# Feed-forward blocks but the first: the row of reciprocal roots by memory instead of by transposes, and tile 0 gated behind tile 1's sums

## The chip, the cores and the metric

The kernel runs on one core of one Trainium2 chip. The metric is the device time of one execution in microseconds. The engines are named as in the profile: PE is TensorE (PEld its weight loads), DVE is VectorE, ACT is ScalarE, POOL is GpSimd, SP is SyncE, whose queue issues nearly all transfers here.

## What is computed

Two layers of a decoder trunk for 256 tokens of width 1024, in float32. Each layer is a feed-forward half step, a mixer of three groups of attention heads, and a second feed-forward half step:

```python
def rms_norm(x, g):
    xf = x.astype(jnp.float32)
    y = xf * lax.rsqrt(jnp.mean(xf * xf, axis=-1, keepdims=True) + RMS_EPS)
    return (y * g.astype(jnp.float32)).astype(x.dtype)

def swiglu(x, w_gate, w_up, w_down):
    return (jax.nn.silu(x @ w_gate) * (x @ w_up)) @ w_down

for l in range(DEPTH):
    h = h + 0.5 * swiglu(rms_norm(h, ffn1_norm[l]), ffn1_w_gate[l], ffn1_w_up[l], ffn1_w_down[l])
    h = h + hybrid_mixer(rms_norm(h, mix_norm[l]), w_in[l], ...)
    h = h + 0.5 * swiglu(rms_norm(h, ffn2_norm[l]), ffn2_w_gate[l], ffn2_w_up[l], ffn2_w_down[l])
```

The hidden width of the feed-forward steps is 2816. So there are four feed-forward blocks in a run: two per layer, with the mixer between the two of a layer. The reciprocal root in `rms_norm` is one number per token; it is what the change carries in another way.

## The kernel before

**Weights.** Each matrix product in float32 is made from pieces in a rounded format: a weight unit of 128 x 1024 values is loaded raw, ScalarE makes its high part `wh` (L118) and VectorE the rest `wl` (L122). Transfers of 1 MB go into five `raw` buffers (`RAW_BUFS`); a buffer's next load is issued by SyncE (L92) as soon as both units in it are split. Up to eight split units are kept. `W.pump()` emits the next split of each kind, and where it stands in the program is where the split stands in the queues of ScalarE and VectorE. The order on each engine is the order of the program; there is no scheduler (`manual_schedule`).

**Feed-forward block.** The hidden width is cut into 22 tiles of 128 columns (`NF`). For each tile a `Pair` of PSUM banks takes the gate and the up product, hidden columns on the partitions and the 256 tokens along the free axis. `wide` is eight matmuls with `wh` on 512 columns for each of the two banks, `narrow` eight with `wl` on 256 columns; odd tiles do the narrow ones first (`swapped`). The banks have four buffers, so tile f + 2 takes the banks of tile f. `summed` (L441 on ScalarE, L442 on VectorE) adds the two halves of a bank and so frees it. Then `gated` multiplies by the reciprocal roots `norm.rb` (L446, VectorE) and takes the tanh (L448, ScalarE); `silu` is two operations of VectorE (L465, and L466 with `rb` again); `hidden` multiplies by the up half (L453), makes the high part `hh` (L456, ScalarE) and the rest `hl` (L459, VectorE). The down product of tile f - 4 is done in the loop at tile f (`DOWN_LAG`), in four `acc` banks.

**The norm.** The products run on the input that is not yet divided by its root mean square; the reciprocal roots come in at `gated` and `silu`. Squares are summed while the first products run. `norm.sums` (L358, L313 on VectorE, L314 on GpSimd) gives `self.r`, named `y_n` in the profile: token p of half t on partition p, column t. The tiles need it along the free axis and on all partitions, as `rb`, 128 x 256. `norm.broadcast` does that: two transposes on TensorE of a column of `y_n` spread over 128 columns (L364), and a copy from PSUM by ScalarE (L366).

**Head of a block.** Tiles 0 and 1 start together, `p0` and `p1`, while the second half of the input is still turned (L338). Then: `norm.sums`, the rest of `p0`, `summed` of tile 0, the rest of `p1`'s wide products, `norm.broadcast`, `p1`'s narrow products, and then tile 0 is gated, before the loop over tiles 1 to 21 begins; tile 1's sums are taken as its first step. `W.pump()` stands between the steps of tile 0. The first block of the run (`first`) has an opening of its own; the other three share this head.

Of the kernel before, what the change touches and what calls it, by code (L numbers as in the profile page):

```python
# [10 lines left out]
F32 = mybir.dt.float32  # L11
# [7 lines left out]
P = 128  # L19
S = 256  # L20
# [122 lines left out]
def kernel(ctx: ExitStack, tc: tile.TileContext, x, ffn1_norm, ffn1_w_gate, ffn1_w_up, ffn1_w_down,  # L143
                      mix_norm, w_in, forget_bias, a_q_norm, a_k_norm, b_q_norm, b_k_norm, c_q_norm, c_k_norm,
                      w_out, ffn2_norm, ffn2_w_gate, ffn2_w_up, ffn2_w_down, const, out):
    nc = tc.nc
# [3 lines left out]
    xp = ctx.enter_context(tc.tile_pool(name="xp", bufs=1))  # L150
# [2 lines left out]
    sm = ctx.enter_context(tc.tile_pool(name="sm", bufs=4))  # L153
    at = ctx.enter_context(tc.tile_pool(name="at", bufs=1))
    pp = ctx.enter_context(tc.tile_pool(name="pp", bufs=2))
    psum = ctx.enter_context(tc.tile_pool(name="psum", bufs=4, space=PSUM))
    ctx.enter_context(tc.manual_schedule())

# [2 lines left out]
    def bank(tag):  # L161
        return psum.tile([P, 512], F32, name="ps_" + tag, tag=tag)

    def tmp(n):
        return tp.tile([P, 512], F32, name="tmp", tag="tmp")[:, :n]
# [39 lines left out]
    W = Weights(tc, raw_pool, split_pool)  # L205
# [74 lines left out]
    def load_small():  # L280
        nc.sync.dma_start(cst, const)
        load_gains(1, mix_norm, nc.sync)
        load_gains(2, ffn2_norm, nc.sync)
        nc.sync.dma_start(fb, bass.AP(tensor=forget_bias.tensor, offset=forget_bias.offset,
                                      ap=[[0, P], [8, DEPTH], [1, 8]]))
# [19 lines left out]
    def mm3(o, lhs, rhs, start, stop):  # L305
        mm(o, lhs[0], rhs[0], start, False)
        mm(o, lhs[0], rhs[1], False, False)
        mm(o, lhs[1], rhs[0], False, stop)
# [8 lines left out]
    class Norm:  # L317
# [43 lines left out]
        def broadcast(self):  # L361
# [3 lines left out]
            self.rb = xp.tile([P, S], F32, name="rb", tag="rb")  # L365
            A.copy(self.rb, ps[:, :S])  # L366

    def tokens(o, q, hid, w, start, stop, cols=slice(0, 512)):

        t, c = q % 2, q // 2  # L370
        mm3(o, [h[:, t * P:(t + 1) * P] for h in hid], [v[:, 0, 512 * c + cols.start:512 * c + cols.stop] for v in w],
            start, stop)
# [8 lines left out]
    def ffn(norm, nxt, aside=None, first=False):  # L381
        hid = {}

        def down(k):
            w = W.take()
            for q in range(4):
                tokens(acc[q], q, hid[k], w, k == 0, False)
            del hid[k]

        def finish(ks):  # L390
            ws = [(k, W.take()) for k in ks]
            dst = out[0].rearrange("(t p) d -> p t d", p=P)
            for q in range(4):
                for c in ((0, 512),) if q < 3 else ((0, 256), (256, 512)):
                    c = slice(*c)
                    o = bank("gu")[:, :S] if c.start else acc[q][:, c]
                    if c.start:
                        residual(q, acc[q][:, c], 0.25, c)
                    for k, w in ws:
                        tokens(o, q, hid[k], w, c.start > 0 and k == ks[0], k == ks[-1], c)  # L400
                    d = residual(q, o, 0.25, c)
                    at = 512 * (q // 2) + c.start
                    nc.sync.dma_start(dst[:, q % 2, at:at + c.stop - c.start], d)
# [34 lines left out]
        def summed(ps):  # L438

            o = tmp(S)  # L440
            A.copy(o, ps[:, 1])  # L441
            V.tensor_tensor(o, ps[:, 0], o, op=ALU.add)  # L442
            return o

        def gated(t_):
            V.tensor_tensor(t_, t_, norm.rb, op=ALU.mult)  # L446
            th = tmp(S)
            A.activation(th, t_, AF.Tanh, scale=0.5)  # L448
            return t_, th

        def hidden(f, t_, th, u, pumps=1):
            late = f >= NF - 2
            V.tensor_tensor(t_, u, t_, op=ALU.mult)  # L453
            hh = hp.tile([P, S], F32R, name="hh", tag="hh")
            hl = hp.tile([P, S], F32R, name="hl", tag="hl")
            (V.tensor_copy if late else A.copy)(hh, t_)  # L456
            if not late:
                W.pump(pumps)
            V.tensor_tensor(hl, t_, hh.bitcast(F32), op=ALU.subtract)  # L459
            if late:  # L460
                W.pump(pumps)
            hid[f] = (hh, hl)

        def silu(t_, th):
            V.scalar_tensor_tensor(t_, th, 1.0, t_, op0=ALU.add, op1=ALU.mult)  # L465
            V.tensor_tensor(t_, t_, norm.rb, op=ALU.mult)  # L466
# [87 lines left out]
            p1.both(lo)  # L554
        W.pump()
        norm.sums()
        (g0, u0), (g1, u1) = p0.both(hi), p1.ps
        W.pump()
        g0, u0 = summed(g0), summed(u0)
        W.pump()  # L560
        p1.wide(hi)
        norm.broadcast()
        p1.narrow(hi)
        W.pump()
        t_, th = gated(g0)
        if not first:
            W.pump()
        silu(t_, th)
        hidden(0, t_, th, u0, int(not first))
        acc = [bank("acc") for _ in range(4)]  # L570
        for f in range(1, NF):
            last = f == NF - 1
            def lagging():
                if DOWN_LAG <= f != NF - 2:
                    down(f - DOWN_LAG - last)

            if f == 1:
                g, u = g1, u1
            elif f % 2:
                g, u = Pair().swapped(lagging)  # L580
            else:
                p = Pair()
                p.wide(range(KT))
                lagging()
                p.narrow(range(KT))
                g, u = p.ps
            if last:
                W.pump()
            g = summed(g)
            if not last:  # L590
                u = summed(u)
            t_, th = gated(g)
            if last:
                W.low()
                down(f - DOWN_LAG)
            else:
                W.pump()
                if f == 1:
                    lagging()
                if f >= DOWN_LAG:  # L600
                    W.pump()
            silu(t_, th)
            hidden(f, t_, th, summed(u) if last else u, 3 if last else 1 + (first and f in (2, 3)))
            if f == 4 and first:
                load_small()
            if f == 8 and aside:
                aside()
# [3 lines left out]
    def tail(acc, rhs, ks, factor, make_norm, late=None):  # L611

        nxt = make_norm()
        ws = dict(zip(ks, [W.take() for _ in ks]))

        def part(q, some):
            for k in some:
                tokens(acc[q], q, rhs[k], ws[k], False, k == ks[-1])  # L620

        ahead = [0] * 4
        if late:
            part(0, ks[:2])
            part(1, ks[:1])
            late()
            part(1, ks[1:2])
            part(2, ks[:1])
            ahead = [2, 2, 1, 0]
        for q in range(4):  # L630
            part(q, ks[ahead[q]:])
            residual(q, acc[q], factor)
            if q == 2:
                nxt.half(0)
        W.pump()
        return nxt
# [548 lines left out]
    def before_mixer(l):  # L1185
        if l == 0:
            turn_gains(1)
            turn_gains(2)
            V.tensor_copy(identr, ident)
            V.memset(causal[:, P:2 * P], 0.0)  # L1190
            for t in range(2):
                V.tensor_scalar(causal[:, 2 * t * P:(2 * t + 1) * P], future, NEG, None, op0=ALU.mult)
        mixer_tables(l)
# [8 lines left out]
    norm = Norm(0, 0)  # L1202
    turn_gains(0)
    for l in range(DEPTH):
        norm = ffn(norm, lambda: Norm(1, l), lambda: before_mixer(l), l == 0)
        norm = mixer(l, norm, lambda: Norm(2, l))
        norm = ffn(norm, (lambda: Norm(0, l + 1)) if l + 1 < DEPTH else None)
# [35 lines left out]
```

## Time and profile before

| What | us |
|---|---|
| median of 3 runs | 1037.53 |
| lowest and highest run | 1037.35, 1038.41 |
| profiled execution | 1037.25 |
| span of the profiled execution | 1035.5 |
| PE busy | 1031.3 |
| DVE busy | 808.0 |
| ACT busy | 592.1 |
| POOL busy | 147.3 |

The profile is one execution. Its page gives the busy time of each engine, the granted clock of TensorE in 40 slices (9 is full), and the chain that ended last, followed back from the last instruction. The timeline gives instructions in order of time: start and length in microseconds, engine, line, operation, destination and source, count, and in brackets the idle time of the engine just before and what ended it. Instructions that follow each other and are alike stand in one row with a count, so the length of such a row is that of the group. Matmuls are pipelined and overlap: the distance between starts, not the length, is what one costs. The rows of transfers give count, size, and the time from issue to landing.

### The profile page before, as it was taken

How to read it: one execution, taken by the hardware profiler on the slowest of the kernel's cores; microseconds unless marked ns; L12 is line 12 of the kernel's file. 1: busy time of each engine (PE TensorE's matmuls, PEld its weight loads, DVE VectorE, ACT ScalarE, POOL GpSimd, SP SyncE). 2: the span in 40 equal slices, each digit the busy share in tenths (PEclk: the TensorE clock that was granted, in tenths of full speed). 3: DMA queues.
4: the chain of work that ended last, by engine and by line, in shares of the span. 5: the costliest groups of instructions: out<-in, count | busy, mean ns of one | idle time of the engine just before them, and what ended most of it. 6: DMA issues, size and time to landing. Idle time of an engine off the chain costs nothing.

```text
span 1035.5 us, 15082 instructions
## 1 busy us (share of the span) xinstructions
PE 1031.3 (100%) x5641; PEld 898.4 (87%) x5641; DVE 808.0 (78%) x1537; ACT 592.1 (57%) x1045; POOL 147.3 (14%) x177
## 2 busy tenths in 40 slices
PE   9999999999999999999999999999999999999998
PEld 8888888898888888888888888888988988888887
DVE  6977778789876877777788777787898768777776
ACT  6655556666854655555465555557676646555552
POOL 2003000167800000000000110002766000000000
PEclk9999999999999999999999999999999999999999
DMA  9664656554431364645645564664455224564631
GB/s 324 224 240 162 208 188 198 182 191 170 158 127 42 123 230 150 230 168 203 198 163 193 182 224 146 241 186 172 164 195 170 83 69 160 180 204 162 236 130 41
DMA packets 130808, 181.61 MB, mean 175 GB/s; under 512 B 7040, under 2 KB 104624, under 8 KB 130736
## 3 DMA queue, kind: packets, MB, share of 16 engines
q1 hardware_dynamic: 130704, 180.66, 51.3%
q8 instruction: 44, 0.72, 0.3%
q14 instruction: 28, 0.23, 0.1%
q10 hardware_dynamic: 32, 0.01, 0.0%
HBM read 179.60 MB, written 1.05 MB: 174 GB/s over the span
## 4 chain that ended last, share of the span: by engine, by line
PE 100%; DVE 0%; POOL 0%; issue 0%; POOLq 0%
PE ps_gu L303 66%; PE ps_acc L303 30%; PE ps_acc L338 1%; PE ps_gu L1037 1%; PE ps_gu L1140 1%; PE ps_acc L738 0%; PE ps_acc L1037 0%; PE ps_gu L1070 0%; PE ps_acc L495 0%; PE ps_acc L364 0%; PE ps_acc L1070 0%; PE ps_gu L179 0%; DVE trunk L377 0%; POOL ones L183 0%; POOL minus_half L185 0%
## 5 line engine op out<-in xcount | busy, mean ns | idle before, releaser
L122 DVE TENSOR_TENSOR wl<-raw,wh 128x1024 fp32r<-128x1024 f32 (+2 forms) x342 | 417.0, 1225 | 24.7 <-ACT wh L118 24.7
L118 ACT CAST wh<-raw 128x1024 fp32r<-128x1024 f32 (+2 forms) x341 | 343.1, 1036 | 5.4 <-PE ps_gu L303 4.8
L303 PE MATMUL ps_gu<-xhl,wh 128*128 128x512 f32 x1408 | 330.2, 390 | 0.0
L303 PEld LDWEIGHTS ps_gu<-xhl,wh 128*128 128x128 f32 x1408 | 262.7, 188 | 53.8 <-ACT wh L118 0.3
L303 PEld LDWEIGHTS ps_gu<-xhl,wl 128*128 128x128 f32 x1408 | 176.0, 191 | 4.3 <-issue 0.2
L303 PE MATMUL ps_gu<-xhl,wl 128*128 128x256 f32 x1408 | 179.2, 283 | 0.1
L303 PE MATMUL ps_gu<-wh,xhl 128*128 128x512 f32 (+2 forms) x512 | 157.2, 377 | 0.0
L442 DVE TENSOR_TENSOR tmp<-ps_gu,tmp 128x256 f32<-128x256 f32 x176 | 73.0, 423 | 107.8 <-ACT tmp L441 107.5
L303 PE MATMUL ps_acc<-wh,hh 128*128 128x512 f32 (+1 forms) x352 | 137.2, 390 | 0.0
L303 PE MATMUL ps_acc<-wl,hh 128*128 128x512 f32 (+1 forms) x352 | 137.0, 389 | 0.0
L303 PE MATMUL ps_acc<-wh,hl 128*128 128x512 f32 (+1 forms) x352 | 136.5, 388 | 0.0
L441 ACT COPY tmp<-ps_gu 128x256 f32<-128x256 f32 x176 | 63.5, 371 | 93.5 <-PE ps_gu L303 93.2
L303 PEld LDWEIGHTS ps_gu<-wh,xhl 128*128 128x128 f32 x512 | 94.8, 188 | 14.6
L456 ACT CAST hh<-tmp 128x256 fp32r<-128x256 f32 x80 | 32.6, 407 | 119.7 <-DVE tmp L453 119.7
L303 PE MATMUL ps_gu<-wl,xhl 128*128 128x512 f32 (+2 forms) x256 | 95.7, 374 | 0.0
L448 ACT ACTIVATE tmp<-tmp 128x256 f32<-128x256 f32 x88 | 36.9, 419 | 82.3 <-DVE tmp L446 81.9
L314 POOL TENSOR_TENSOR y_n<-msq,minus_half 128x2 f32<-128x2 f32 x6 | 6.8, 1141 | 530.9 <-DVE msq L313 530.9
L303 PEld LDWEIGHTS ps_acc<-wh,hl 128*128 128x128 f32 x352 | 66.1, 188 | 13.9
L303 PEld LDWEIGHTS ps_acc<-wh,hh 128*128 128x128 f32 x352 | 66.2, 188 | 12.6
L303 PEld LDWEIGHTS ps_acc<-wl,hh 128*128 128x128 f32 x352 | 66.2, 188 | 12.2
L303 PEld LDWEIGHTS ps_gu<-wl,xhl 128*128 128x128 f32 x256 | 48.2, 188 | 6.7
L327 ACT ACTIVATE xhl<-ps_acc,gT 128x256 fp32r<-128x256 f32 x48 | 19.1, 474 | 38.7 <-PE ps_acc L338 35.6
(221 smaller groups left out, 1000.4 us busy)
## 6 DMA issues: line engine op xcount, KB each, us to landing
raw<-in_ffn_w_down_dram SPq DMA_DIRECT2D x44, 1024.0 KB, 4.9
raw<-in_ffn_w_gate_dram SPq DMA_DIRECT2D x42, 1024.0 KB, 6.6
raw<-in_ffn_w_up_dram SPq DMA_DIRECT2D x42, 1024.0 KB, 7.3
raw<-in_w_in_dram SPq DMA_DIRECT2D x24, 1024.0 KB, 4.9
raw<-in_w_out_dram SPq DMA_DIRECT2D x8, 1024.0 KB, 4.9
raw<-in_w_in_dram SPq DMA_DIRECT2D x4, 768.0 KB, 4.9
raw<-in_w_in_dram SPq DMA_DIRECT2D x4, 656.0 KB, 3.9
raw<-in_ffn_w_gate_dram SPq DMA_DIRECT2D x3, 512.0 KB, 7.0
```

The costliest lines, as they stand in the source:

```text
L118: self.nc.scalar.copy(hv, src)
L122: (engine or self.nc.vector).tensor_tensor(lv, self.srcs[self.n_low], hv.bitcast(F32), op=ALU.subtract)
L303: T.matmul(o, l, r, start=start, stop=stop, skip_group_check=True)
L314: G.tensor_tensor(y, dst, minus_half[:, :n], op=ALU.pow)
L327: A.activation(self.h[:, m], src, AF.Copy, scale=gT[:, self.col + m:self.col + m + 1])
L338: T.transpose(ps[:, i, t * P:(t + 1) * P], trunk[:, t, (2 * mp + i) * P:(2 * mp + i + 1) * P], ident)
L441: A.copy(o, ps[:, 1])
L442: V.tensor_tensor(o, ps[:, 0], o, op=ALU.add)
L448: A.activation(th, t_, AF.Tanh, scale=0.5)
L456: (V.tensor_copy if late else A.copy)(hh, t_)
L1037: T.transpose(b[:, j * P:(j + 1) * P], pj[i][:, j * P:(j + 1) * P], ident)
L1140: T.transpose(b[:66, i * S + t * P:i * S + (t + 1) * P], src[t][:, 2 * hp_ + i, :], ident)
```

## The change

In the three blocks after the first, `norm.broadcast` is not called. A new method `spread` is called right after `norm.sums`: it writes `self.r` to a row of 256 numbers in memory, in the order of the tokens, and then reads that row back to all 128 partitions, with two transfers on SyncE's queue. The read waits for the write to land. The three `W.pump()` that stood between and behind `gated`, `silu` and `hidden` of tile 0 are emitted at once after `p1.narrow`, and tile 0's `gated`, `silu` and `hidden` move into the loop's first step, behind `summed` of both halves of tile 1.

```diff
+    dram = ctx.enter_context(tc.tile_pool(name="dram", bufs=1, space=bass.MemoryType.DRAM))
...
+        def spread(self):
+
+            row = dram.tile([2, P], F32, name="r_row", tag="r_row")
+            self.rb = xp.tile([P, S], F32, name="rb", tag="rb")
+            nc.sync.dma_start(row.rearrange("t p -> p t"), self.r)
+            nc.sync.dma_start(self.rb, bass.AP(tensor=row.tensor, offset=row.offset, ap=[[0, P], [1, S]]))
...
         W.pump()
         norm.sums()
+        if not first:
+            norm.spread()
         (g0, u0), (g1, u1) = p0.both(hi), p1.ps
         W.pump()
         g0, u0 = summed(g0), summed(u0)
         W.pump()
         p1.wide(hi)
-        norm.broadcast()
+        if first:
+            norm.broadcast()
         p1.narrow(hi)
-        W.pump()
-        t_, th = gated(g0)
-        if not first:
-            W.pump()
-        silu(t_, th)
-        hidden(0, t_, th, u0, int(not first))
+        W.pump(1 if first else 3)
+
+        def tile0():
+            t_, th = gated(g0)
+            silu(t_, th)
+            hidden(0, t_, th, u0, 0)
+
+        if first:
+            tile0()
         acc = [bank("acc") for _ in range(4)]
         for f in range(1, NF):
...
             g = summed(g)
             if not last:
                 u = summed(u)
+            if f == 1 and not first:
+                tile0()
             t_, th = gated(g)
```

Lines of the changed kernel stand 8 to 16 further down from `spread` on; `gated`'s product with `rb`, L446 before, is L454.

## The prediction

> **What bounds the kernel now.** I read the page first, then the chain of waits, then the order of time around each place that the diff touches.
>
> ```profile
> span 1035.5 us, 15082 instructions
> PE 1031.3 (100%) x5641; PEld 898.4 (87%) x5641; DVE 808.0 (78%) x1537; ACT 592.1 (57%) x1045; POOL 147.3 (14%) x177
> PEclk9999999999999999999999999999999999999999
> PE 100%; DVE 0%; POOL 0%; issue 0%; POOLq 0%
> ```
>
> TensorE (PE) is busy for 1031.3 of 1035.5 us at full granted clock, and the chain that ended last is TensorE work from end to end. Only two things can move the end: matmul work that goes away, and a gap that opens in the stream. All idle time of TensorE in the span is 4.2 us, so nothing that fills gaps can be worth more than that.
>
> The edit concerns three of the four feed-forward blocks; they begin near 336, 520 and 849 us. I call them B2, B3 and B4. Here is TensorE at the head of each (start, length, engine, line, operation, count):
>
> ```profile
> 342.49 2.00 PE L303 MATMUL ps_gu<-xhl,wh 128*128 128x512 f32 x8
> 345.28 2.00 PE L303 MATMUL ps_gu<-xhl,wh 128*128 128x512 f32 x8
> 347.12 0.38 PE L364 MATMUL ps_acc<-ident,y_n 128*128 128x128 f32 x2
> 347.26 1.20 PE L303 MATMUL ps_gu<-xhl,wl 128*128 128x256 f32 x8
> 348.30 3.82 PE L303 MATMUL ps_gu<-xhl,wh 128*128 128x512 f32 x16
> 351.95 4.00 PE L303 MATMUL ps_gu<-xhl,wl 128*128 128x256 f32 x32
> 355.78 7.44 PE L303 MATMUL ps_gu<-xhl,wh 128*128 128x512 f32 x32
> ...
> 526.63 2.00 PE L303 MATMUL ps_gu<-xhl,wh 128*128 128x512 f32 x8
> 529.42 2.00 PE L303 MATMUL ps_gu<-xhl,wh 128*128 128x512 f32 x8
> 532.43 3.82 PE L303 MATMUL ps_gu<-xhl,wh 128*128 128x512 f32 x16
> 539.92 7.44 PE L303 MATMUL ps_gu<-xhl,wh 128*128 128x512 f32 x32
> ...
> 858.04 2.00 PE L303 MATMUL ps_gu<-xhl,wh 128*128 128x512 f32 x8
> 861.05 3.82 PE L303 MATMUL ps_gu<-xhl,wh 128*128 128x512 f32 x16
> 868.54 7.44 PE L303 MATMUL ps_gu<-xhl,wh 128*128 128x512 f32 x32
> ```
>
> The reader sees one stream without a hole, in which each start is the issue time and the lengths overlap.
>
> **Part 1: the transposes leave TensorE.** Eight wide and eight narrow matmuls without transposes go from 342.49 to 345.28: 2.79 us. The next sixteen, with the two transposes between them, go from 345.28 to 348.30: 3.02 us. So the two transposes cost 0.23 us of stream, not their 0.38 us of busy time. In B3 it is 532.43 - 529.42 against 529.42 - 526.63, 3.01 against 2.79; in B4 861.05 - 858.04 = 3.01 against the same 2.79. Sum: 0.23 + 0.22 + 0.22 = 0.67 us, all on the path. The two bounds are 0 (if the slots were filled by something else) and 3 x 0.38 = 1.14 us. I take 0.67 because it is a start-to-start difference. ScalarE's copy of the row out of PSUM (L366) goes too; it is off the path.
>
> **Part 2: the reciprocal roots take two transfers.** They go out on SyncE's queue, behind the row's producer on GpSimd:
>
> ```profile
> 342.59 1.55 POOL L314 TENSOR_TENSOR y_n<-msq,minus_half 128x2 f32<-128x2 f32 x1 [60.87 <-DVE msq L313]
> 526.00 0.70 POOL L314 TENSOR_TENSOR y_n<-msq,minus_half 128x2 f32<-128x2 f32 x1 [181.86 <-DVE msq L313]
> 855.35 1.54 POOL L314 TENSOR_TENSOR y_n<-msq,minus_half 128x2 f32<-128x2 f32 x1 [60.86 <-DVE msq L313]
> 347.56 0.37 SPq L92 DMA_DIRECT2D raw<-in_ffn_w_gate_dram  x1
> 523.38 0.37 SPq L92 DMA_DIRECT2D raw<-in_ffn_w_down_dram  x1
> 532.75 0.37 SPq L92 DMA_DIRECT2D raw<-in_ffn_w_gate_dram  x1
> raw<-in_ffn_w_down_dram SPq DMA_DIRECT2D x1, 1024.0 KB, 7.4
> out_dram<-trunk SPq DMA_DIRECT2D x2, 128.0 KB, 1.8
> raw<-in_w_in_dram SPq DMA_DIRECT2D x4, 16.0 KB, 3.7
> 69.98 0.37 SPq L92 DMA_DIRECT2D raw<-in_ffn_w_up_dram  x1
> 73.38 0.43 SPq L200 DMA_DIRECT2D gb<-in_c_k_norm_dram  x1
> raw<-in_ffn_w_up_dram SPq DMA_DIRECT2D x1, 1024.0 KB, 7.6
> gb<-in_c_k_norm_dram SPq DMA_DIRECT2D x1, 32.0 KB, 8.4
> ```
>
> The roots are ready at 344.14, 526.70 and 856.89. First transfer, 256 single values to memory: the nearest rows are the last output writes (128 KB in 1.8 us, large pieces) and the 16 KB loads in 32-byte pieces (3.7 us, behind a large load). I take 2.3: 1.8 plus half a microsecond, my estimate for 256 pieces; ends 1.8 and 3.7, though no piece in the trace is as small as 4 bytes. Second transfer, 1 KB read 128 times, 128 KB in all: the nearest form is the gains, each 256 bytes read 128 times. The load ahead of the six gains landed at 69.98 + 7.6 = 77.6, the last gain at 73.38 + 8.4 = 81.8, so six took 4.2 us, 0.7 each. If that is a matter of pieces, rb needs 0.7 + 1.8 = 2.5 us; if of bytes, 4 x 0.7 + 1.8 = 4.6. I take the long end, 4.6, since each piece of rb is four times a gain's; ends 1.8 and 4.6. With 0.1 us for each wait on SyncE the row arrives 0.1 + 2.3 + 0.1 + 4.6 = 7.1 us after the roots, at 351.2 and 864.0. In B3 a load of 1 MB is still in the rings; it lands at 523.38 + 7.4 = 530.8. The row follows them, say 531.0, and rb lands at 531.0 + 0.1 + 4.6 = 535.7.
>
> SyncE now waits inside this pair, and the next weight loads stand behind it (347.56 in B2, 532.75 in B3, which wait for a free buffer anyway). rb is issued at 344.14 + 2.5 = 346.6 and at 531.1, before those loads come due, so none is moved at the values taken; at the long end of the first transfer one load goes out about half a microsecond late, while the buffers ahead of it hold the units for the next tiles.
>
> **Part 3: tile 0 goes behind tile 1's sums.** VectorE's new order at the head of a block is: four splits wl in a row, the two sums of tile 1, five operations of tile 0, five of tile 1, then tile 2's sums. No split is added or lost; there were four before tile 1's sums already, but spread over tile 0's operations.
>
> ```profile
> 345.81 1.05 ACT L118 CAST wh<-raw 128x1024 fp32r<-128x1024 f32 x1
> 346.28 2.35 DVE L122 TENSOR_TENSOR wl<-raw,wh 128x1024 fp32r<-128x1024 f32 x2
> 353.07 0.76 DVE L442 TENSOR_TENSOR tmp<-ps_gu,tmp 128x256 f32<-128x256 f32 x2 [0.22 <-ACT tmp L441]
> 353.75 0.41 DVE L446 TENSOR_TENSOR tmp<-tmp,rb 128x256 f32<-128x256 f32 x1
> 356.46 0.42 DVE L459 TENSOR_TENSOR hl<-tmp,hh 128x256 fp32r<-128x256 f32 x1 [0.47 <-ACT hh L456]
> 356.81 0.75 DVE L442 TENSOR_TENSOR tmp<-ps_gu,tmp 128x256 f32<-128x256 f32 x2
> 537.88 0.42 DVE L446 TENSOR_TENSOR tmp<-tmp,rb 128x256 f32<-128x256 f32 x1
> 541.16 0.43 DVE L459 TENSOR_TENSOR hl<-tmp,hh 128x256 fp32r<-128x256 f32 x1 [0.47 <-ACT hh L456]
> ```
>
> B2: the splits start at 346.28 and four take 4 x 1.17 = 4.7 us, to 351.0. ScalarE makes its four wh from 345.81, at 1.05 each, to 350.0, and then copies tile 1's halves, so it is done about when VectorE gets there. The sums take 353.75 - 353.07 = 0.68, and tile 0's first use of rb stands at 351.7: 7.55 us after the roots, against 7.1 needed. rb is hidden. B3 runs as B2 does, 532.43 - 348.30 = 184.13 us later, B4 861.05 - 348.30 = 512.75: there the first use falls at 535.8 (rb lands at 535.7, just in time) and at 864.4 (864.0).
>
> Who waits for VectorE next? Tile 3 uses the PSUM banks of tile 1: before, tile 1's sums began at 353.07 and tile 3's narrow matmuls at 351.95 + 1.92 = 353.87, a margin below a microsecond; now these sums are done by 351.7 and the margin grows. Tile 4 uses the banks of tile 2, and there it shrinks. From L446 to the start of L459 a tile takes 356.46 - 353.75 = 2.71 us, and the next operation starts 0.35 later. Tile 0 at 351.7, tile 1 at 354.76, its L459 at 357.47, tile 2's first sum from 357.82 to 358.24. Tile 4 begins 16 matmuls into the row of 355.78, each (351.95 - 348.30) / 16 = 0.228: at 359.4, or 359.2 with the transposes gone. Margin 0.95 us in B2, the same in B4. In B3 one split stays inside tile 1 (541.16 - 537.88 = 3.28 us instead of 2.71): 535.8 + 3.06 + 3.28 + 0.35 + 0.42 = 542.9, against 539.92 + 3.65 - 0.22 = 543.35: margin 0.45 us. So tile 1 and tile 2 run late by one to two microseconds and TensorE doesn't notice; without this cover each microsecond of VectorE's delay would be one of TensorE's. Tile 0's own product is wanted only behind the 32 matmuls of 355.78, near 363 us.
>
> **The sum.** Profiled execution: 1037.25 (span 1035.5 and 1.75 around it) - 0.67 = 1036.58. The median shown is 0.28 above that execution, 1037.53, so the forecast for the median is 1036.9.
>
> **The rivals.**
> Rival A, slower: the second transfer is slow, because 128 reads of one kilobyte go at the pace of the gains' tail. In the gains' stretch (slices of 0.16 us) several in a row stand near 20 GB/s:
>
> ```profile
> GB/s 342 241 162 120 102 74 84 36 41 120 77 24 22 17 22 17 22 3 0 0 27 81 120 57 20 17 16 0 19 22 24 21 25 3 0 0 0 0 0 0
> ```
>
> 131 KB at 20 GB/s are 6.6 us, with 1.8 fixed 8.4: rb lands 10.9 us after the roots, 3.35 late, and VectorE stands in order with sums and splits queued behind the waiting L454. Less the margin that is 2.4 us of TensorE in B2 and in B4; in B3 531.1 + 8.4 = 539.5, 3.7 late, 3.25 left. Sum 8.05 - 0.67 = 7.4 us slower: 1044.9. It decides as soon as both transfers together take more than 7.55 + 0.95 = 8.5 us in B2 and B4, or rb lands after 536.25 in B3. Against it: the same view shows 120 GB/s in between, so the average is twice as good.
> Rival B, slower by less: the first transfer pays for its 256 pieces of 4 bytes, an eighth of the smallest pieces in the rows above, and takes 4.6 us, twice what I took. rb then lands 0.1 + 4.6 + 0.1 + 4.6 = 9.4 us after the roots: 1.85 late, 0.9 lost in B2 and B4; in B3 2.3 later than taken, 538.0, 1.75 lost. Sum 3.55 - 0.67 = 2.9 slower: 1040.4. Against it: the first transfer would have to pass its long end of 3.7 while the second stands at its own. The Trainium skill speaks for it: "DMA: Bandwidth & Descriptors", section "Rules for kernel authors", has one descriptor per element where the last dimension is strided, and counts transposing by a rearranged pattern 19 times worse than the hardware's transpose. With that page's 10.5 ns per packet and 2.0 us fixed, 256 pieces come to 4.7 us (an estimate from the page). No row of this trace can show it.
> Rival C, no gain: VectorE's walk is longer than mine by about a microsecond (waits for ScalarE inside tile 0), and B3's thin margin gives back 0.4 to 1 us: 1037.3 to 1037.9. For it: a margin of 0.45 us that rests on rows merged two by two. Against: the same intervals serve for before and after.
> Rival D, faster: the earlier sums of tile 1 free banks and remove more than the transposes. It would need half of the 4.2 us of idle time, and the stream above shows none of it in these places; 1035.3.
>
> **How the numbers follow.** Forecast 54%, Rival C 20%, Rival B 11%, Rival A 11%, Rival D 4%. A measurement of this kernel can tell about 0.2%, 2.1 us, from no change. Forecast and C lie inside it (74%), A and B outside (22%), D below (4%). For the range: low end 1036.2, close to where the transposes are worth their full 1.14 us (1036.4); high end 1040.6, which takes in Rival B and leaves out A and D, 15%. The forecast's own range is 1036.2 to 1037.5.
>
> **What would show it.** Right: no L364 with x2 in B2, B3 and B4; tile 2's wide matmuls 2.79 us after the last wide ones of tile 1; landing of rb at most 4.6 us from issue; VectorE's L454 of tile 0 (L446 before) at about 351.5 us without a long wait for a transfer; no gap on TensorE before tile 4. Wrong: a wait on the transfer of rb longer than 1 us on VectorE, or a hole in TensorE's stream within 15 us behind the sums.

## The result and the profile after

| What | before | after |
|---|---|---|
| median of 5 runs, us | 1037.53 | 1060.63 |
| lowest and highest, us | 1037.35, 1038.41 | 1060.12, 1061.43 |
| span of the profiled execution, us | 1035.5 | 1058.9 |
| PE busy, us | 1031.3 | 1038.4 |

The changed kernel is slower by 23.1 us; the ratio of the times is 1.0222, with a 95% interval from 1.0211 to 1.0233. The forecast was 1036.9.

The page of the changed kernel, first the busy times of its engines, the granted clock and the shares of the chain that ended last, then two rows of its transfers (size, and median time from issue to landing):

```profile
PE 1038.4 (98%) x5635; PEld 902.8 (85%) x5635; DVE 808.3 (76%) x1537; ACT 590.9 (56%) x1042; POOL 147.6 (14%) x177
...
PEclk9999999999999899999998999999999999999999
...
PE 92%; DMA 4%; DVE 2%; ACT 1%; issue 0%; POOL 0%; POOLq 0%; DVEq 0%; ACTq 0%
...
r_row<-y_n SPq DMA_DIRECT2D x3, 1.0 KB, 7.7
rb<-r_row SPq DMA_DIRECT2D x3, 128.0 KB, 6.3
```

The six transposes are gone (5641 matmuls before, 5635 now), and yet PE's busy time grew by 7 us: some matmuls became longer. Two slices of the clock show 8 in place of 9. Transfers now hold 4% of the chain. The chain through the head of B2, in order of time, says which (start, length, what):

```profile
342.69 1.56 POOL y_n L315
...
344.26 7.48 DMA r_row<-y_n
...
351.76 6.70 DMA rb<-r_row
...
358.55 0.44 DVE tmp L454
...
365.20 6.81 PE ps_gu L304 x16
```

Row and read stand in series, 14.2 us where the prediction had 7.1. Tile 0's product with rb (L454), both tiles' gating and tile 2's sums (L450) follow, and then TensorE starts tile 4. Its stream around the three places, with the wide matmuls of tiles 1 and 2 in B2 ahead of them, to be held against the rows 355.78, 539.92 and 868.54 of before, where 32 wide matmuls of tiles 3 and 4 ran in one row of 7.44 us:

```profile
345.38 2.00 PE L304 MATMUL ps_gu<-xhl,wh 128*128 128x512 f32 x8
...
348.17 3.82 PE L304 MATMUL ps_gu<-xhl,wh 128*128 128x512 f32 x16
...
355.66 3.81 PE L304 MATMUL ps_gu<-xhl,wh 128*128 128x512 f32 x16
365.20 6.81 PE L304 MATMUL ps_gu<-xhl,wh 128*128 128x512 f32 x16 [5.72 <-DVE tmp L450]
371.84 0.39 PE L304 MATMUL ps_acc<-wh,hh 128*128 128x512 f32 x1
...
548.48 3.81 PE L304 MATMUL ps_gu<-xhl,wh 128*128 128x512 f32 x16
557.28 6.39 PE L304 MATMUL ps_gu<-xhl,wh 128*128 128x512 f32 x16 [4.99 <-DVE tmp L450]
563.51 0.39 PE L304 MATMUL ps_acc<-wh,hh 128*128 128x512 f32 x1
...
884.64 3.82 PE L304 MATMUL ps_gu<-xhl,wh 128*128 128x512 f32 x16
894.01 5.34 PE L304 MATMUL ps_gu<-xhl,wh 128*128 128x512 f32 x16 [5.56 <-DVE tmp L450]
899.19 0.39 PE L304 MATMUL ps_acc<-wh,hh 128*128 128x512 f32 x1
```

Each row of 32 is torn between tile 3 and tile 4. Sixteen wide matmuls cost 3.65 us in the stream of before (348.30 to 351.95). The hole runs from 355.66 + 3.65 to 365.20 in B2, 5.89 us; it is 5.15 in B3 and 5.72 in B4, 16.8 in all. Behind the hole the same sixteen take 6.64, 6.23 and 5.18 us, so 2.99, 2.58 and 1.53 more than 3.65, 7.1 in all. 16.8 + 7.1 - 0.67 for the transposes is 23.2, against the 23.1 measured. Nothing else is needed for the sum. The windows view of the stretches behind the first two holes gives the granted clock in its third column from the end:

```profile
365.20:371.84 6.64, 6.64 (x16) 5.21 (x17) 6.36 (x12) 4.04 (x8) 0.00 (x0) 0.53 0.19 51
557.28:563.50 6.22, 6.22 (x16) 4.88 (x17) 5.93 (x12) 3.60 (x8) 0.00 (x0) 0.57 0.16 26
```

0.53 and 0.57, where every slice of before shows 9; the same view gives 0.70 for B4 (894.01 to 899.19). What the traces alone do not say: why 1 KB takes 7.5 to 8.5 us to reach memory, why the read takes 6.1 to 6.7, and whether the move of tile 0 has a share.

### The profile page after: what moved, and what is told of

Same layout as the page of the kernel before. It is cut to its first block, busy times and chain, and to the rows that moved or that the text cites. A ratio compares the mean times of both kernels' runs of the same rounds, so it can differ in the third digit from the quotient of the medians.

```text
span 1058.9 us, 15069 instructions
## 1 busy us (share of the span) xinstructions
PE 1038.4 (98%) x5635; PEld 902.8 (85%) x5635; DVE 808.3 (76%) x1537; ACT 590.9 (56%) x1042; POOL 147.6 (14%) x177
## 3 DMA queue, kind: packets, MB, share of 16 engines
HBM read 179.99 MB, written 1.05 MB: 171 GB/s over the span
## 4 chain that ended last, share of the span: by engine, by line
PE 92%; DMA 4%; DVE 2%; ACT 1%; issue 0%; POOL 0%; POOLq 0%; DVEq 0%; ACTq 0%
PE ps_gu L304 60%; PE ps_acc L304 29%; DMA r_row<-y_n 2%; DMA rb<-r_row 2%; PE ps_gu L1053 1%; PE ps_acc L339 1%; PE ps_gu L1156 1%; DVE wl L122 1%; PE ps_acc L754 0%; PE ps_acc L1053 0%; PE ps_gu L1086 0%; DVE tmp L461 0%; DVE tmp L474 0%; DVE xhl L331 0%; DVE hl L467 0%
## 5 line engine op out<-in xcount | busy, mean ns | idle before, releaser
L304 PE MATMUL ps_gu<-xhl,wh 128*128 128x512 f32 x1408 | 337.8, 396 | 16.3 <-DVE tmp L450 16.3
L304 PEld LDWEIGHTS ps_gu<-xhl,wh 128*128 128x128 f32 x1408 | 267.4, 191 | 72.9 <-DVE tmp L450 17.5
L450 DVE TENSOR_TENSOR tmp<-ps_gu,tmp 128x256 f32<-128x256 f32 x176 | 72.8, 422 | 108.2 <-ACT tmp L449 107.8
L304 PEld LDWEIGHTS ps_gu<-wh,xhl 128*128 128x128 f32 x512 | 94.8, 188 | 14.6
L454 DVE TENSOR_TENSOR tmp<-tmp,rb 128x256 f32<-128x256 f32 x88 | 37.0, 421 | 19.4 <-DMA rb<-r_row 19.3
```

The lines of the kernel that those rows point to most:

```text
L304: T.matmul(o, l, r, start=start, stop=stop, skip_group_check=True)
```

## The experiments

The kernel before was timed again beside each of three batches, on one chip each: 1037.15 us (the order alone, filling the hole, more cover, first probes), 1037.50 (the transfers alone, second probes, breaking the series, the row collected) and 1037.09 (third probes, the spacing alone, the hops on GpSimd). Ratios and differences below are to the before of the same batch, where nothing else is said.

**The order alone.** The changed kernel with the transposes kept in all blocks, so that only the order of tile 0 and the splits is left:

```diff
-        if not first:
-            norm.spread()
...
-        if first:
-            norm.broadcast()
+        norm.broadcast()
```

> The move of tile 0 alone; the roots still go by transposes in every block. Theory L (the two transfers take about 14 us, VectorE stands in order behind them, tile 4 finds its banks full, and TensorE first stands still and then runs at half clock): the move costs nothing, 1037.0 to 1038.0, no gap on TensorE before tile 4. Rival R (tile 0's late gating is itself part of the loss): above 1040, a gap before tile 4 without any transfer.

Measured: 1037.12 us, ratio 1.0000 (0.9991 to 1.0009). VectorE in B2:

```profile
351.61 0.41 DVE L454 TENSOR_TENSOR tmp<-tmp,rb 128x256 f32<-128x256 f32 x1
...
357.79 0.75 DVE L450 TENSOR_TENSOR tmp<-ps_gu,tmp 128x256 f32<-128x256 f32 x2
```

Part 3 of the prediction had tile 0 at 351.7 and tile 2's first sum at 357.82. The move costs nothing by itself.

**The transfers alone.** The kernel before with `spread` in place of the transposes, but tile 0 still gated ahead of tile 1's sums:

```diff
         norm.sums()
+        if not first:
+            norm.spread()
...
-        norm.broadcast()
+        if first:
+            norm.broadcast()
```

> The kernel before with its row of roots spread through memory as in the change, but tile 0 still gated ahead of tile 1's sums. If rb lands some 14 us after the roots here too, tile 1's sums come only behind tile 0's gating, 3 to 4 us after rb, and tile 3, which needs tile 1's banks, starts some 10 us late in each of the three blocks, with 1.5 to 3 us more for the lower clock after the gap: 1068 to 1080. By the rival that the move of tile 0 is what costs the time, this is faster than the changed kernel: 1037 to 1050.

Measured: 1072.24 us, ratio 1.0334 (1.0313 to 1.0354). TensorE in B2:

```profile
351.97 2.07 PE L304 MATMUL ps_gu<-xhl,wl 128*128 128x256 f32 x16
363.71 3.78 PE L304 MATMUL ps_gu<-xhl,wl 128*128 128x256 f32 x16 [9.67 <-DVE tmp L450]
```

The hole opens some 5.4 us earlier than in the changed kernel (353.9 against 359.3), in the middle of tile 3's narrow matmuls, and is 9.67 us long, as expected. The other two are 7.74 and 9.73 us. So the move takes 11.6 us off the damage (34.7 against 23.1, each beside its own before); the whole loss is the transfers'.

**Filling the hole.** The changed kernel with 26 matmuls into a bank of `acc`, whose values the first real product overwrites, ahead of tile 4 in the three blocks:

```diff
+            if f == 4 and not first:
+                for _ in range(26):
+                    mm(acc[0].rearrange("p (a b) -> p a b", a=2), norm.h[:, 0, 0:P], norm.x[:, 0], True, True)
```

> The changed kernel with 26 extra matmuls of 512 columns between tiles 3 and 4 in the three blocks, about 5.9 us each time, whose result is thrown away (the down product's first matmul starts the bank anew). Theory L: they take the place of the gap (5.9, 5.2 and 5.7 us), the clock stays at full, and the 7.1 us that tile 4's wide matmuls lost at the lower clock come back: 1053.5 to 1054.5. Rival C (tile 4's wide matmuls are slow for another reason, such as their data): 1060 to 1062.

Measured: 1055.75 us. TensorE in B2:

```profile
359.20 6.05 PE L304 MATMUL ps_acc<-xhl 128*128 128x512 f32 x26
365.44 3.96 PE L304 MATMUL ps_gu<-xhl,wh 128*128 128x512 f32 x16 [0.18 <-DVE tmp L450]
```

Tile 4 starts 0.24 us later than in the changed kernel, and its sixteen matmuls are back from 6.81 to 3.96, at a granted clock of 1.00. The time is 1.3 us above the expected range: in B3 the filling is longer than the hole was, and in B4 TensorE still waits 0.69 us behind it. With the filling, 6.24, 5.89 and 6.74 us lie between tile 3 and tile 4, 18.9 in all, against holes of 16.8. 18.9 - 0.67 is 18.2, and 18.6 was measured. The lower clock is a consequence of the hole and worth 7.1 us.

**More cover.** The changed kernel with tiles 0 and 1 gated behind tile 2's sums, tiles 2 and 3 behind tile 3's:

```diff
-            if f == 1 and not first:
-                tile0()
+            if f in (1, 2, 3) and not first:
+                held.append((f, g, u))
+                W.pump(2)
+                if f == 1:
+                    continue
+                if f == 2:
+                    tile0()
+                while len(held) > 1 or f == 3 and held:
+                    i, g, u = held.pop(0)
...
+                continue
```

> The changed kernel with tiles 0 and 1 gated behind tile 2's sums, and tiles 2 and 3 behind tile 3's sums, in the three blocks: the banks are freed before VectorE waits for rb. Theory L: both transfers still land 14 us after the roots, nothing on TensorE waits, and only the transposes' 0.67 us are left: 1036.5 to 1037.5. Rival R, or a further cost of the transfers (weight loads held up on SyncE behind them): above 1039, with a gap on TensorE somewhere else.

Measured: 1038.12 us, ratio 1.0010 (1.0001 to 1.0019). The transfers are no faster (VectorE's row of B2, first use of rb):

```profile
359.33 0.42 DVE L454 TENSOR_TENSOR tmp<-tmp,rb 128x256 f32<-128x256 f32 x1 [2.15 <-DMA rb<-r_row]
```

rb still comes near 359, but no PSUM bank waits for it, and 22.1 of 23.1 us come back. The time is 0.6 us above the expected range, and the gain of Part 1 doesn't show: 0.97 us over before in place of 0.67 under it. Of these 1.6 us the trace shows 0.86, a wait of TensorE for a split (`wl`, in B2); the rest is not traced.

**Transfers by themselves, first probes.** The kernel before, with transfers whose data nobody reads, in the quiet stretches of the two mixers and in the heads of blocks; among them:

```diff
+            nc.sync.dma_start(line.rearrange("t p c -> p t c")[:, :, 0:1], trunk[:, :, 0:1])
+            nc.sync.dma_start(row[0:2 * P].rearrange("(p t) -> p t", t=2), trunk[:, 0, 0:2])
...
+            nc.sync.dma_start(line.rearrange("t p c -> p t c")[:, :, 0:16], trunk[:, :, 0:16])
```

> The kernel before with extra transfers that nobody waits for, one behind the other where the rings are idle; only their landing times matter. Out to memory: 1 piece of 1 KB; 256 pieces of 4 bytes, each to a place of its own 512 bytes apart; 128 pieces of 8 bytes side by side; 256 of 64 bytes; 256 of 512 bytes. In from memory: 1 KB read 128 times, just written and, in another place, a constant. Inside SBUF: 256 pieces of 4 bytes from 128 partitions into one. Theory P (the small pieces make the write to memory slow): 512 bytes land in about 2 us, 64 bytes in less than 4, the 4-byte pieces in 7 wherever they go, 8 bytes in between. Rival S (neighbouring pieces from different rings share a line of memory): the spread 4-byte pieces land in 2 to 3 us, the dense 8-byte ones in 5 or more. Rival N (the number of pieces): all of 256 pieces land alike in 6 to 8. For the read: about 6 us for both if the repeated reading of one kilobyte is slow, about 2.5 for the constant if it is the fresh write.

Measured: 1037.03 us. SyncE's queue in the first mixer; each of these waits for the one above it, so that starts give the landings:

```profile
308.93 0.38 SPq L403 DMA_DIRECT2D line<-trunk  x1
310.53 0.34 SPq L404 DMA_DIRECT2D line<-trunk  x1
313.46 0.33 SPq L388 DMA_DIRECT2D got<-line  x1
```

256 pieces of 4 bytes, 512 bytes from one to the next, land in 1.6 us. 128 pieces of 8 bytes side by side take 2.9. The broadcast read takes 3.0 here. In the second mixer 256 pieces of 64 bytes take 1.6 and of 512 bytes 3.2. So neither the number of pieces nor their 4 bytes is the cause. Rival S is the nearest to what the later probes show, but it missed too: it had 5 us or more for the dense 8-byte pieces. The read of a constant took 4.8, behind a 1 MB load. Inside SBUF 256 values reach one partition in 1.9 us; they went as 128 pieces of 8 bytes, not as the 256 of 4 that the expectation names.

**Second probes: the change's own row.** The same, with the dense row of the change and two spacings:

```diff
+            nc.sync.dma_start(row[0:S].rearrange("(t p) -> p t", t=2), trunk[:, :, 0])
...
+            nc.sync.dma_start(row[0:S * 16].rearrange("(t p c) -> p t c", t=2, c=16)[:, :, 0:1], trunk[:, :, 0:1])
+            nc.sync.dma_start(line.rearrange("t p c -> p t c")[:, :, 0:1], trunk[:, :, 0:1])
```

> The kernel before, with transfers whose data nobody reads put into quiet stretches: in the first mixer a piece of 1 KB, then the same dense row of 256 neighbouring 4-byte pieces that the change writes, then the broadcast read of it with no load behind; in the second mixer a piece of 1 KB, 256 4-byte pieces 64 bytes apart, 256 pieces 512 bytes apart, then the broadcast read; and in the second feed-forward block the dense row from the roots, at its own place, with nobody waiting. By the theory that neighbouring 4-byte pieces get in each other's way in memory, the dense row takes 6 to 9 us in both places, the row at 64 bytes something from 1.6 to 6, the row at 512 bytes 1.6. By the rival that the row is slow only at its place (a load of 1 MB just ahead of it, the roots just written), the dense row takes 1.6 to 2.3 us in the quiet stretch and 7 to 8 at its own place. For the second transfer: if it is slow because loads stand right behind it, both broadcast reads take 3.0 us; if it is slow because its line was just written in dense pieces, the first takes 6 and the second 3. The time is that of before, 1036.5 to 1038.5.

Measured: 1037.46 us. SyncE's queue in the two mixers:

```profile
309.54 0.38 SPq L399 DMA_DIRECT2D line<-trunk  x1
317.26 0.34 SPq L388 DMA_DIRECT2D got<-line  x1
...
822.41 0.37 SPq L401 DMA_DIRECT2D line<-trunk  x1
823.98 0.36 SPq L402 DMA_DIRECT2D line<-trunk  x1
826.50 0.34 SPq L388 DMA_DIRECT2D got<-line  x1
```

The dense row takes 317.26 - 309.54 = 7.7 us with nothing near it, and 8.9 us from the roots at its own place; the same 256 pieces 64 bytes apart take 1.57. Those 512 bytes apart took 2.5 this time, not the 1.6 of the first probes; that is a scatter of about one microsecond in single readings. So it is not the place that makes the dense row slow, but how near its pieces lie to each other. The read behind the spaced rows landed in 2.9 us; for the one behind the dense row the trace has no landing, only data until about 4.7 us after its issue, with no load near it.

**Third probes: spacings between, and half a row.** Spacings of 32, 16 and 8 bytes, and a dense row of 128 values:

> The kernel before with transfers whose data nobody reads: in the first mixer's quiet stretch a piece of 1 KB, then 256 pieces of 4 bytes with 32, 16 and 8 bytes from one to the next, then the broadcast read; in the second mixer's a piece of 1 KB, then 128 neighbouring pieces of 4 bytes, half of the change's row, then the broadcast read. If pieces that share 64 bytes of memory wait for each other, with (7.7 - 1.6) / 15 = 0.4 us for each further piece of a line, then 32 bytes apart (2 in a line) takes 2.0 us, 16 bytes (4) 2.8, 8 bytes (8) 4.4, and the half row, 16 in a line, 7.7 as the whole. By the rival that the cost grows with the number of all such pieces, the half row takes 4 to 5 us. By the rival that only pieces that touch are slow, 8 bytes apart takes 1.6 us. The time is that of before, 1036.5 to 1038.5.

Measured: 1036.94 us. SyncE's queue in the first mixer (32, 16, 8 bytes apart, then the read), and the row of the view of transfers for the half row in the second:

```profile
309.18 0.38 SPq L397 DMA_DIRECT2D line<-trunk  x1
311.29 0.36 SPq L398 DMA_DIRECT2D line<-trunk  x1
314.24 0.36 SPq L399 DMA_DIRECT2D line<-trunk  x1
317.21 0.34 SPq L388 DMA_DIRECT2D got<-line  x1
```

```profile
line<-trunk SPq DMA_DIRECT2D x1, 0.5 KB, 6.9
```

2.1, 2.9 and 3.0 us, against the 2.0, 2.8 and 4.4 expected; the half row takes 6.9, nearly the time of the whole, against 7.7 expected. So it isn't the total of pieces that counts, but how near they lie to each other: 64 bytes apart costs 1.6, 32 costs 2.1, 16 and 8 cost 2.9 to 3.0, 4 costs 6.9 to 7.7. That the pieces which share 64 bytes wait for each other is not shown: the straight line of 0.4 us a piece misses at 8 bytes, and the steps from 1.6 to 3.0 are hardly larger than the scatter of one microsecond. The one step that is clear of it lies between 8 and 4 bytes, so 4-byte values that share 8 bytes would fit as well. The reads took 3.8 behind the pieces 8 bytes apart and 4.9 behind the dense half row, again with no load behind them.

**The spacing alone, in the changed kernel.** The decisive one: same transfers, same count, same waits, only each value 64 bytes from the next. (The read therefore fetches 1 KB in which only 16 of the 256 values were just written.)

```diff
-            row = dram.tile([2, P], F32, name="r_row", tag="r_row")
-            nc.sync.dma_start(row.rearrange("t p -> p t"), self.r)
+            nc.sync.dma_start(row.rearrange("t p c -> p t c")[:, :, 0:1], self.r.rearrange("p (t c) -> p t c", c=1))
...
+    row = dram.tile([2, P, 16], F32, name="r_row", tag="r_row")
```

> The changed kernel with the same first transfer, 256 pieces of 4 bytes behind the same wait and at the same place of the queue, but each piece put 64 bytes from the next in memory (a scratch array, filled once in the first mixer). The read of rb is unchanged, 1 KB in one stretch to each partition, behind the same wait; it therefore carries other numbers than the roots, and the output is not the reference's. By the theory that it is the neighbourhood of the pieces alone that costs the time, the row takes 1.6 to 2.3 us (4 to 5 in the third block, where a load of 1 MB stands ahead), rb 3 to 4.3, no gap ahead of tile 4 but perhaps 1 us in the third block, and the time is 1036.4 to 1038.7: 22 to 24 of the 23 us come back. By the rival that the place makes the row slow (roots just written, loads ahead, SP's wait), it takes over 6 us as before and the time is 1055 to 1062.

Measured: 1036.39 us beside 1037.09 of before, ratio 0.9994 (0.9984 to 1.0003). The transfers of B2, and SyncE's queue and VectorE's first use in B3:

```profile
rb<-r_row SPq DMA_DIRECT2D x1, 128.0 KB, 3.1
r_row<-y_n SPq DMA_DIRECT2D x1, 1.0 KB, 1.9
```

```profile
526.27 0.37 SPq L372 DMA_DIRECT2D r_row<-y_n  x1
531.06 0.34 SPq L373 DMA_DIRECT2D rb<-r_row  x1
532.33 0.37 SPq L92 DMA_DIRECT2D raw<-in_ffn_w_gate_dram  x1
...
535.16 0.41 DVE L455 TENSOR_TENSOR tmp<-tmp,rb 128x256 f32<-128x256 f32 x1
```

All that was lost comes back. The median is 0.70 us below before, though the interval reaches just past no change. No hole, no lower clock. The read, too, is at 2.9 to 3.1 us in all three blocks. That does not settle why it took 6.1 to 6.7 in the changed kernel, because two things differ: here it is not the line just written densely that is read, and the next weight load goes out 1.3 to 1.9 us behind the read, there 0.45 (352.21 - 351.76). The other runs show a share for each. With no load behind, the read takes 2.9 after pieces 512 bytes apart, and 4.7 or more and 4.9 after dense ones; with loads 0.5 us behind and a row written as one piece (the repair below) it takes 4.1 to 4.2.

**Breaking the series.** The changed kernel with rb read from a constant of the input, so that it needn't wait for the row, which is still written densely:

```diff
-            nc.sync.dma_start(self.rb, bass.AP(tensor=row.tensor, offset=row.offset, ap=[[0, P], [1, S]]))
+            nc.sync.dma_start(self.rb, bass.AP(tensor=const.tensor, offset=const.offset, ap=[[0, P], [1, S]]))
```

> The changed kernel with the second transfer reading the first 1 KB of a constant input in place of the row, so that it no longer waits for the first, which is still written; the factors are then other numbers than the roots. If the loss hangs on the two hops in series, the read is issued some 0.4 us after the row's write and lands 3 to 7 us later, before the first use at 7.55 us: no gap ahead of tile 4, and 1036.4 to 1037.8. By the rival that the read alone, with loads right behind it, would have been late in any case, it takes over 7.5 us and the time is 1040 or more.

Measured: 1039.05 us, ratio 1.0015 (1.0005 to 1.0026). The transfers in B2:

```profile
raw<-in_ffn_w_gate_dram SPq DMA_DIRECT2D x1, 1024.0 KB, 10.5
raw<-in_ffn_w_up_dram SPq DMA_DIRECT2D x1, 1024.0 KB, 12.7
rb<-in_const_dram SPq DMA_DIRECT2D x1, 128.0 KB, 8.1
r_row<-y_n SPq DMA_DIRECT2D x1, 1.0 KB, 8.3
```

21.6 of 23.1 us come back, so the series was most of the loss. The time lies between the two expected ranges; in the profiled execution, the fastest of its eight runs, TensorE waits once in the three heads, 0.69 us ahead of tile 4 in B4. But the letter of the rival came true: the read alone took over 7.5 us, 8.1 to 8.7 in the three blocks. It has no dependence on the row and stands 0.4 us behind it in the queue, and it lands with it; the loads behind the pair, issued at nearly the same times as with the spaced row, take 10.5 and 12.7 us where they took 5.3 and 7.0 there (10.7 and 12.5 against 6.0 and 7.5 in B4; 7.0 and 8.6 against 5.4 and 7.4 in B3, where they go out 6 us behind the row). The dense write holds up what is queued behind it.

**Repairs with the right values.** The row collected inside SBUF first, written to memory as one piece, then read:

```diff
+            line = xp.tile([P, S], F32, name="line", tag="line")
+            for t in range(2):
+                nc.sync.dma_start(line[0:1, t * P:(t + 1) * P], self.r[:, t:t + 1])
-            nc.sync.dma_start(row.rearrange("t p -> p t"), self.r)
+            nc.sync.dma_start(row.rearrange("t p -> (t p)"), line[0:1])
```

> The changed kernel with the row collected first inside SBUF, into one partition (two transfers of 128 pieces, one per tile of tokens, side by side), then written to memory as one piece of 1 KB, then read by all partitions as in the change. By the theory of the dense pieces: 1.9 us for the collection (as in the first probes), 1.6 to 2 for the piece, and 3.0 to 6.7 for the read, 6.5 to 10.6 us after the roots against the 7.55 that the first use leaves. With the read at 3 to 4 us rb is hidden and the time is 1036.4 to 1037.5; with the read at 6.1 to 6.7, rb is some 2.5 us late, the margin of 0.5 to 1.0 takes off a part, and the time is 1040 to 1045. By the rival that the row is slow at its place whatever its pieces, the collection takes 5 us or more and the time is 1050 to 1065.

Measured: 1038.77 us, ratio 1.0014 (1.0004 to 1.0023). SyncE's queue in B2 and TensorE in B3:

```profile
343.87 1.18 SPq L375 DMA_DIRECT2D line<-y_n  x2
346.51 0.31 SPq L376 DMA_DIRECT2D r_row<-line  x1
347.64 0.37 SPq L377 DMA_DIRECT2D rb<-r_row  x1
```

```profile
544.06 3.92 PE L304 MATMUL ps_gu<-xhl,wh 128*128 128x512 f32 x16 [1.05 <-DVE tmp L453]
```

In B2 and B4 the two collecting transfers land in 1.9 to 2.0 us each, but 2.6 and 2.9 us pass from the first issue to the next hop, because the second goes out behind the first. The piece takes 1.1 to 1.2, the read 4.1 to 4.2: between the two cases expected. In B3 the collection stands behind a 1 MB load (4.9 us) and TensorE waits 1.05 us, more than the transposes were worth. With the same three hops issued by GpSimd (`nc.gpsimd` for `nc.sync`):

> The version with the row collected inside SBUF, with its three hops issued by GpSimd, which writes the roots itself, in place of SyncE: their queue holds no loads, and SyncE's loads no longer stand behind the hops' waits. If the third block's late collection (4.9 us, behind a 1 MB load in the same queue) was all that was left of the loss, the hops take 2.0 + 1.1 + 3 to 4.3 us in all three blocks, rb is hidden, and the time is 1036.4 to 1037.6. By the rival that a transfer issued by GpSimd costs that engine more than a microsecond each, or shares the DMA engines with loads that now start earlier, rb lands 9 us or more after the roots and the time is 1039 to 1050.

Measured: 1056.67 us, ratio 1.0189 (1.0172 to 1.0206), worse than either theory had it. GpSimd's queue in B2, and TensorE's tile 4 there:

```profile
347.56 0.52 POOL L376 DMA_DIRECT2D r_row<-line  x1 [1.91 <-DMA line<-y_n]
351.81 0.58 POOL L377 DMA_DIRECT2D rb<-r_row  x1 [3.73 <-DMA r_row<-line]
```

```profile
362.64 5.43 PE L304 MATMUL ps_gu<-xhl,wh 128*128 128x512 f32 x16 [3.38 <-DVE tmp L453]
```

The issue costs GpSimd about half a microsecond each, but the one piece now takes 4.0 us in B2 and B4 in place of 1.1. SyncE no longer holds back its weight loads behind the hops, and they move at the same time. B3 fits this: there the piece goes out just ahead of the loads and takes 1.6 us, and the read, just behind them, takes 6.1 (4.1 and 4.7 in the other blocks). That the loads are the cause is still a reading, not tried. A hole of 3.4 us already brings the lower clock (5.43 for sixteen matmuls, granted clock 0.70).

## Why the prediction was wrong

**Part 1 (transposes, 0.67 us): right.** In the changed kernel tile 2's wide matmuls stand 348.17 - 345.38 = 2.79 us behind tile 1's in B2, and 2.79 in B3 and B4 as well, where before it was 3.01 to 3.02. With the transfers out of the way the change gains 1037.09 - 1036.39 = 0.70 us; the runs alone would not tell so little from nothing, the rows of the trace do.

**Part 2 (transfers): the step that failed.** "First transfer, 256 single values to memory: ... I take 2.3 ... ends 1.8 and 3.7" measured 7.5 to 8.5 us, more than twice the long end. The prediction weighed the size of a piece and the number of pieces; it did not see that what counts here is that they lie side by side in memory. The same 256 pieces spaced out take 1.5 to 1.9 us at the same place (4.8 in B3 behind its load, landing at 531.06, where the prediction had 531.0). "Second transfer ... 4.6" measured 6.1 to 6.7, past its long end; behind the spaced row it takes 2.9 to 3.1, below the value taken. Part of its excess follows from the first transfer's form (4.7 to 4.9 behind dense pieces with no load near, against 2.9 behind pieces 512 bytes apart), and part can come from the loads close behind it (4.1 to 4.2 behind the single piece). In B2 no packet of it moves from 351.8 to 354.8. What it waits for there stays open, and so does what the memory does with the dense pieces.

Of the rule of the Trainium skill that Rival B named, the runs bear out the loss and not the reason: the estimate of 4.7 us for 256 pieces is too long for spaced pieces (1.6) and too short for dense ones (7.7). The Trainium skill, "DMA: Bandwidth & Descriptors", section "Specifications", says that transfers below 512 bytes are done as read-modify-write. Pieces of 4 bytes that lie 64 bytes apart show no price for it here (1.5 to 1.9 us, as 1.6 for pieces of 64 bytes); whether it is what makes the dense ones slow, no run here shows.

**Part 3 (order and margins): right, to 0.1 us.** Take the prediction's own formula with the measured landings. In B2 rb lands 351.76 + 6.70 - 344.25 = 14.2 us after the roots; less 7.55 for the first use and 0.95 of margin, TensorE should stop for 5.7 us. The profile says 5.72. In B3 the row goes out at 535.46 and lands at 543.94, the read takes 6.1: 14.6 us, less 535.8 - 526.7 = 9.1 and 0.45, 5.05, where the profile has 4.99. B4: 7.7 + 6.3 less 8.5, 5.5 where it has 5.56. The order alone costs nothing, and without it the loss is 34.7 us.

**A missing term.** The prediction and all its rivals priced a hole by its length. The clock behind it added 7.1 of 23.2 us, and filling the hole took that away. The Trainium skill describes it in "TensorE: Matmul & The Clock Gate", Part 1: about 3.4 us without work bring half the clock until about 3.4 us of work have gone by. The trace agrees on half the clock: right behind each of the three holes it is 0.50. On how long it lasts the trace agrees only in B4: from the means of 0.53, 0.57 and 0.70 over the sixteen matmuls it is 6.2 us in B2, 5.3 in B3 and 3.1 in B4 (an estimate that takes the clock as either 0.50 or 1).

**The rivals.** Rival A named the late read as the cause (8.4 us; 6.1 to 6.7 measured) and Rival B the slow write (4.6; 7.5 to 8.5 measured). Both were true at once, which neither had, and the sum of the two hops, 14.2 us in B2, passed Rival A's point of 8.5 by far. So no rival came near the 1060.6 either; Rival A's 1044.9 was the highest. Rival C's longer walk did not occur. Rival D's idle time was not there, and no version with right values was found that is faster than the kernel before; the most that there is to gain is the 0.7 us.

**The signs named beforehand.** "a wait on the transfer of rb longer than 1 us on VectorE, or a hole in TensorE's stream" were the two signs of a wrong forecast, and both are there: waits of 6.9 us at most, idle times of 5.0 to 5.7. Of the signs for a right one only those of Part 1 came: no transposes in the three blocks, and 2.79 us.

## What to carry to other kernels

A transfer that turns a column into a row is not priced by its bytes or its pieces alone: look at where the pieces land, and measure the very form, before it is put on a path with half a microsecond of margin. Two hops through memory in series need their sum hidden, at their worst and behind whatever load stands ahead in the queue. A hole of several microseconds in TensorE's stream costs more than its length; count the matmuls behind it at about half the clock, here for 3.1 to 6.2 us.

## What the hardware showed that was not expected

- 256 values of 4 bytes written side by side to memory take 7.7 us in a quiet stretch, 64 bytes apart 1.57 us, and half as many side by side still 6.9 us.
- Such a write holds up transfers queued behind it that have nothing to do with it: a read of 128 KB from elsewhere lands after 8.1 to 8.7 us in place of 2.9 to 3.1, and 1 MB loads in B2 after 10.5 and 12.7 us in place of 5.3 and 7.0.
- During most of that time nothing of the row moves: in the view of transfers of B2 its 272 packets pass near 345.2 us, and the landing comes at 344.26 + 7.48 = 351.74. The spaced row's 272 packets pass near 345.0, and it lands at 343.96 + 1.9 = 345.9. So the packets take no longer (about 0.25 us in both); what is late is the landing.
